# Hybrid HGRN2 / FNet layer: two gate tiles of the conv MLP copied from PSUM to SBUF pages ahead of their conv

## The chip, the cores and the metric

One core of a Trainium2 chip runs the whole program. The time of a run is the device time in microseconds (us); several runs are taken and the median is quoted. A profile is one more execution, with its own time, recorded by the hardware profiler. Engines are called PE (TensorE), PEld (its weight load), DVE (VectorE), ACT (ScalarE), POOL (GpSimd) and SP (SyncE).

## What is computed

One layer on 1024 tokens of width 1024: a token mixer (a gated linear recurrence beside a Fourier mixer), a residual, then a gated MLP with a 3x3 depthwise conv on the gate branch, another residual, and a final RMSNorm. The change lies in the MLP:

```python
def conv_ffn(h, w_up, w_dw, b_dw, w_down, rows, cols):
    a, u = jnp.split(h @ w_up, 2, axis=-1)
    a = lax.conv_general_dilated(a.reshape(B, rows, cols, D_FF), w_dw..., padding=((1, 1), (1, 1)), feature_group_count=D_FF)
    a = a.reshape(B, L, D_FF) + b_dw
    return (jax.nn.gelu(a) * u) @ w_down
```

D_FF is 2816, that is 22 tiles of 128 columns; the grid is 16 rows of 64 tokens.

## The kernel before

Everything is kept transposed: a tile of D_FF columns is 128 partitions by 1024 tokens, gate (`a`) and value (`u`) alike. Each float32 matrix product is made of three matmuls on rounded high and low parts, so every operand is split by `split` (L61 to L63: ACT casts the high part, DVE subtracts it to get the low part).

**Two plain tiles.** The tiles ff = 0 and 1 (`PLAIN = 2`) are computed directly by `plain` (L862), and this work keeps PE busy while norm2 of the second token half is still being made (L745 to L804). The gate columns of such a tile are gathered in a two-bank PSUM tile `psg` (`self.up0[ff][0]`), of which there are two; the value columns go to two one-bank tiles `psm` (four in all) and are copied by ACT to a page `uu` (L803). The gate columns stay in `psg`.

**The twenty other tiles** (loop at L884) use a 2x2 Strassen-like scheme of seven products, each of twelve matmuls (`product`, L854), here named by their weights: A11, A12, S2, S1, S3, S4, A22, in this order on PE. Their sums are closed by ACT copies out of `psm` ("snaps", L889 to L904, recorded at L939) and two DVE additions that write the gate columns into a `psg` tile: L893 (first half, after A12) and L908 (second half, after S4). L893 of tile ff = 2 takes the `psg` buffer that plain tile 0 had, that of ff = 3 the one of tile 1. The second product of a tile, A12, needs a free `psm` buffer; with four of them, A12 of ff = 3 gets the one that L893 of ff = 2 has read.

**The conv** is `gated` (L918): ACT writes the centre tap with the bias into a page `cv` (L922), DVE adds eight shifted taps with scalar_tensor_tensor (L930, in place, 945, 960 or 1008 elements each), reading the gate columns from `psg`; ACT applies gelu (L932), DVE multiplies by `u` (L933) and a DMA stores the page. For the plain tiles the page comes from the common pool `pg` (33 pages of 128x1024), for the others from `cv` (2).

**Loading** of the next tile's weights is `up_load` (L823): DMA, splits on ACT and DVE, and POOL's sums L839 to L842 and the low part L847, which read and write SBUF.

**Order.** The program is written with a tile framework that allots buffers and sets the waits; each engine's queue is ordered at compile time by program order, by readiness in the framework's own forecast, and by the marks `high_priority` (L888 to L911 and L828). On the chip each queue is then worked off strictly in order: what stands behind a waiting instruction waits too.

Of the kernel before, what the change touches and what calls it, by code (L numbers as in the profile page):

```python
# [34 lines left out]
class Kern:  # L35
# [709 lines left out]
    def norm2(self, half, xs, ssacc):  # L745

        nc, V = self.nc, self.nc.vector
        if half == 0:  # L750
            self.B, self.raw = {}, {}
            tag = "g"
        else:
            self.phase("ffn")
            self.upw = [self.up_load(ff) for ff in range(PLAIN)]
            self.up0 = [(self.pst("g"), [self.pst("m")]) for _ in range(PLAIN)]
            self.plain(0, 0, "a")
            tag = "m"
        r = self.token_rstd(ssacc[:, :512], 4, "n2", tag)
        if half:  # L760
            self.plain(0, 0, "u")
        pt = self.pst(tag)
        self.row_bcast(r, 4, pt)
        if half:
            self.plain(1, 0, "au")

        def operand(name, raw=None):
            hi, lo = self.pg(F32R), self.pg(F32R)
            self.B.setdefault(name, []).append((hi, lo))
            if raw is not None:  # L770
                nc.scalar.copy(hi, raw)
                V.tensor_tensor(lo, raw, hi.bitcast(F32), op=SUB)
            return hi, lo

        def block(name, j, kt0):
            raw = self.raw.setdefault(name, {})[j] = self.pg()
            hi, lo = operand(name)
            for i in range(2):
                d = kt0 + i
                q = slice(i * 512, (i + 1) * 512)  # L780
                tmp = self.tile([P, 512], F32, self.tp)
                sh = self.sh2[:, d:d + 1]
                V.scalar_tensor_tensor(tmp, xs[d // 2][:, q], self.a2[:, d:d + 1], pt[:, :512], op0=MUL, op1=MUL)
                nc.scalar.activation(hi[:, q], tmp, AF.Identity, bias=sh)
                V.scalar_tensor_tensor(lo[:, q], tmp, sh, hi[:, q].bitcast(F32), op0=ADD, op1=SUB)
                nc.scalar.activation(raw[:, q], tmp, AF.Identity, bias=sh)
            return raw

        if half == 0:
            for j in range(2):  # L790
                block("B11", j, 2 * j)
            for j in range(2):
                block("B21", j, 4 + 2 * j)
            return
        b12 = [block("B12", j, 2 * j) for j in range(2)]
        b22 = [block("B22", j, 4 + 2 * j) for j in range(2)]
        self.us = []
        for ff in range(PLAIN):
            self.up0[ff][1].append(self.pst("m"))
            self.plain(ff, 1, "au")  # L800
            u = self.pg(F32, "uu")
            for i in range(2):
                nc.scalar.copy(u[:, i * 512:(i + 1) * 512], self.up0[ff][1][i])  # L803
            self.us.append(u)  # L804
        us = []
        for j in range(2):
            u1, u2 = self.pg(F32, "cv"), self.pg()
            V.tensor_tensor(u1, self.raw["B11"][j], b12[j], op=SUB)
            V.scalar_tensor_tensor(u2, u1, -1.0, b22[j], op0=MUL, op1=SUB)
            operand("U2", u2)  # L810
            operand("U1", u1)
            us.append(u2)
        for j in range(2):
            u3 = self.pg(F32, "cv")
            V.tensor_tensor(u3, b22[j], b12[j], op=SUB)
            operand("U3", u3)
        for j in range(2):
            u4 = self.pg(F32, "cv")
            V.scalar_tensor_tensor(u4, us[j], -1.0, self.raw["B21"][j], op0=MUL, op1=SUB)
            operand("U4", u4)  # L820
# [53 lines left out]
    def ffn(self):  # L874
        nc, V = self.nc, self.nc.vector
        self.gd = []
        first = self.tc.high_priority
        h0, h1 = slice(0, 512), slice(512, 1024)
        snap = lambda src, c=1.0: self.copied(self.tile([P, 512], F32, "sn"), src, c)
        self.upw = [self.up_load(PLAIN)]  # L880
        self.B["B12"] = None
        for ff in range(PLAIN):
            self.gated(ff, self.up0[ff][0], self.us[ff])
        for ff in range(PLAIN, NF):  # L884
            w = self.upw.pop(0)
            X, Y = self.pst("m"), self.pst("m")
            self.product(X, w["A11"], "B11", True)
            with first():  # L888
                s1 = snap(X)  # L889
            self.product(Y, w["A12"], "B21", True)  # L890
            pa = self.pst("g")
            with first():
                V.tensor_tensor(pa[:, h0], s1, Y, op=ADD)  # L893
            self.product(X, w["S2"], "U2", False)
            with first():
                sv = snap(X)
            Z = self.pst("m")
            self.product(Z, w["S1"], "U1", True)
            with first():
                s5 = snap(Z)  # L900
            self.product(X, w["S3"], "U3", False)
            u = self.pg(F32, "uu")
            with first():
                s7 = snap(X, -1.0)  # L904
            self.nc.gpsimd.tensor_tensor(u[:, h1], s7, s5, op=SUB)  # L905
            self.product(Z, w["S4"], "B22", False)
            with first():
                V.tensor_tensor(pa[:, h1], sv, Z, op=ADD)  # L908
            self.product(X, w["A22"], "U4", False)
            with first():  # L910
                nc.scalar.mul(u[:, h0], X, -1.0)  # L911
            if ff + 1 < NF:
                self.upw.append(self.up_load(ff + 1))
            self.gated(ff, pa, u)
        self.B = None
        self.down()
# [346 lines left out]


def lay_out(x, c, ctx, c_ctx, w_mod, b_mod, norm1, norm2, w_in, lb_fwd, lb_bwd,
            hgrn_norm, w_out, w_up, w_dw, b_dw, w_down, norm_f):
    A = np.ascontiguousarray
# [45 lines left out]
```

## Time and profile before

| | |
|---|---|
| median of 3 runs | 1223.97 us (1223.35 to 1224.45) |
| the profiled execution's own time | 1221.22 us |
| its span (first to last instruction) | 1219.4 us |
| mean granted TensorE clock, share of full | 0.998 |
| PE busy | 1181.7 us, 97% |
| DVE busy | 917.8 us, 75% |
| ACT busy | 560.2 us, 46% |
| POOL busy | 201.9 us, 17% |

The profiled time lies 2.75 us below the median and 1.8 us above its span. Shares are means over stages of different character: the stage of the change lies between 565 and 680 us of the span, where the plain tiles pass into the loop. A row of the timeline gives start, duration, engine, line, operation, output and input; in brackets stands how long the engine was idle before it and who ended that. Rows that merge several instructions show their count (x4). Successive instructions of an engine overlap a little in the records, so that their spacing is below their duration.

### The profile page before, as it was taken

What the parts mean: (1) busy time and instruction counts of PE and PEld (TensorE: products, weight loads), DVE (VectorE), ACT (ScalarE), POOL (GpSimd) and SP (SyncE); (2) the same over time, 40 slices, a digit from 0 to 9 for tenths busy, and PEclk for the clock granted to TensorE, in tenths of its full rate; (3) what the DMA queues carried; (4) which work ended last, traced back from release to release, by engine and by line L of the source; (5) the groups of instructions that cost most, each with busy time, mean ns of one, the idle gap of its engine ahead of it and who ended that gap; (6) DMA issues with size and microseconds to landing.
All of it is one profiled execution on the core that took longest, in us unless ns stands there. A gap on an engine that the chain in (4) does not pass through costs nothing.

```text
span 1219.4 us, 15862 instructions
## 1 busy us (share of the span) xinstructions
PE 1181.7 (97%) x6156; PEld 989.0 (81%) x6156; DVE 917.8 (75%) x1192; ACT 560.2 (46%) x809; POOL 201.9 (17%) x124
## 2 busy tenths in 40 slices
PE   7999999999998999999999999999999999999997
PEld 4688888888898888888878788888888888788877
DVE  5861858575887467576999888888888898998685
ACT  6534545454431434365544445444443543435552
POOL 0000000000000000001336455464554400000000
PEclk9999999999999999999999999999999999999999
DMA  9531101010246037453022222222212429635643
GB/s 344 224 130 36 35 18 35 18 35 19 87 153 218 10 121 255 168 184 110 19 94 81 110 95 78 87 78 104 87 70 87 141 74 328 243 126 184 211 162 138
DMA packets 57867, 146.23 MB, mean 120 GB/s; under 512 B 5568, under 2 KB 5824, under 8 KB 57792
## 3 DMA queue, kind: packets, MB, share of 16 engines
q1 hardware_dynamic: 57792, 145.22, 34.3%
q8 instruction: 48, 0.79, 0.3%
q14 instruction: 27, 0.22, 0.1%
HBM read 125.27 MB, written 19.92 MB: 119 GB/s over the span
## 4 chain that ended last, share of the span: by engine, by line
PE 62%; DVE 18%; ACT 9%; DMA 5%; issue 5%; SPq 0%; DVEq 0%; ACTq 0%
PE psm L859 24%; PE psm L74 16%; PE psg L74 13%; PE psm L1035 4%; DVE cv L930 4%; PE psg L1035 3%; DVE wl L63 2%; DMA wm<-in_wm_dram 2%; DVE pg L451 1%; DVE pg L930 1%; DVE sl L63 1%; ACT sq L568 1%; ACT L444 1%; ACT L445 1%; DMA ld<-in_wm_dram 1%
## 5 line engine op out<-in xcount | busy, mean ns | idle before, releaser
L930 DVE SCALAR_TENSOR_TENSOR cv<-psg,vec,cv 128x945 f32<-128x945 f32 (+2 forms) x160 | 195.2, 1220 | 24.0 <-ACT cv L922 20.4
L859 PE MATMUL psm<-pg,sh 128*128 128x512 f32 x640 | 197.1, 389 | 0.6 <-ACT sn L939 0.6
L62 ACT CAST wh<-wr 128x1024 fp32r<-128x1024 f32 x78 | 81.9, 1052 | 144.8 <-PE psg L74 39.8
L859 PEld LDWEIGHTS psm<-pg,sh 128*128 128x128 f32 x640 | 120.0, 188 | 25.9 <-ACT sn L939 1.1
L74 PE MATMUL psg<-pg,wh 128*128 128x512 f32 x472 | 134.9, 395 | 0.0
L839 POOL TENSOR_TENSOR ws<-wx 128x512 f32<-128x512 f32 x20 | 28.8, 1441 | 596.4 <-DMA wx<-in_wup_dram 563.1
L63 DVE TENSOR_TENSOR wl<-wr,wh 128x1024 fp32r<-128x1024 f32 x78 | 96.2, 1235 | 40.4 <-ACT wh L62 39.7
L859 PE MATMUL psm<-pg,sl 128*128 128x512 f32 x320 | 124.5, 389 | 0.0
L859 PE MATMUL psm<-pg,wh 128*128 128x512 f32 x320 | 98.6, 389 | 2.8 <-DVE psg L893 2.8
L74 PEld LDWEIGHTS psg<-pg,wh 128*128 128x128 f32 x472 | 87.2, 188 | 16.9
L939 ACT ACTIVATE sn<-psm 128x512 f32<-128x512 f32 x80 | 47.7, 597 | 109.6 <-PE psm L859 109.6
L74 PE MATMUL psg<-wh,pg 128*128 128x256 f32 x512 | 96.4, 287 | 0.9 <-ACT wh L62 0.8
L74 PEld LDWEIGHTS psg<-wh,pg 128*128 128x128 f32 x512 | 80.6, 191 | 1.6 <-ACT wh L62 1.3
L74 PE MATMUL psg<-pg,wl 128*128 128x512 f32 x236 | 79.1, 395 | 0.0
L74 PE MATMUL psg<-wl,pg 128*128 128x256 f32 x256 | 73.0, 286 | 4.4 <-DVE wl L63 4.4
L859 PEld LDWEIGHTS psm<-pg,wh 128*128 128x128 f32 x320 | 60.0, 188 | 15.6 <-DVE psg L893 3.2
L859 PEld LDWEIGHTS psm<-pg,sl 128*128 128x128 f32 x320 | 60.1, 188 | 12.5
L905 POOL TENSOR_TENSOR uu<-sn,sn 128x512 f32<-128x512 f32 x20 | 39.0, 1948 | 180.5 <-ACT sn L939 177.2
L859 PE MATMUL psm<-pg,wl 128*128 128x512 f32 x160 | 62.3, 389 | 0.0
L74 PE MATMUL psm<-pg,pg 128*128 128x128 f32 (+2 forms) x256 | 56.6, 348 | 5.0 <-DVE pg L506 4.7
L221 DVE SCALAR_TENSOR_TENSOR ma<-wm,silu_c,ma 128x512 f32<-128x512 f32 x56 | 42.0, 750 | 18.1 <-DMA wm<-in_wm_dram 17.6
L847 POOL TENSOR_TENSOR sl<-ws,sh 128x1024 fp32r<-128x1024 f32 x20 | 53.4, 2671 | 5.6 <-ACT sh L846 5.6
(376 smaller groups left out, 2622.4 us busy)
## 6 DMA issues: line engine op xcount, KB each, us to landing
wr<-in_wd_dram SPq DMA_DIRECT2D x35, 512.0 KB, 4.0
wm<-in_wm_dram SPq DMA_DIRECT2D x64, 256.0 KB, 2.9
wx<-in_wup_dram SPq DMA_DIRECT2D x22, 512.0 KB, 4.4
wr<-in_wup_dram SPq DMA_DIRECT2D x22, 512.0 KB, 3.6
gd<-cv SPq DMA_DIRECT2D x20, 512.0 KB, 2.6
pg<-gd SPq DMA_DIRECT2D x33, 256.0 KB, 6.2
ld<-in_wm_dram SPq DMA_DIRECT2D x16, 512.0 KB, 8.2
wr<-in_wo_dram SPq DMA_DIRECT2D x16, 512.0 KB, 3.7
```

What stands on the lines that cost most here:

```text
L62: self.nc.scalar.copy(hi, raw)
L63: self.nc.vector.tensor_tensor(lo, raw, hi.bitcast(F32), op=SUB)
L74: self.nc.tensor.matmul(out, lhsT, rhs, start=start, stop=stop)
L221: nc.vector.scalar_tensor_tensor(acc, w, s, acc, op0=MUL, op1=ADD)
L444: nc.scalar.activation(lf, g[d][0], AF.Ln)
L839: G.tensor_tensor(s31[:, hi], u[:, lo], u[:, hi], op=ADD)
L847: G.tensor_tensor(S31[1], s31, S31[0].bitcast(F32), op=SUB)
L859: self.nc.tensor.matmul(out, w[a][:, q], B[kt // 2][b][:, t], start=(first and kt == 0 and j == 0), stop=(kt == 3 and j == 2), skip_group_ ...
L905: self.nc.gpsimd.tensor_tensor(u[:, h1], s7, s5, op=SUB)
L930: V.scalar_tensor_tensor(c3[:, ro, co], a3[:, ri, ci], w9((dr + 1) * 3 + dc + 1), c3[:, ro, co], op0=MUL, op1=ADD)
L939: self.nc.scalar.mul(dst, src, c)
L1035: nc.tensor.matmul(pts[j][:, q], W[a][:, w], G[b][:, i * 512 + q.start:i * 512 + q.stop], start=first and p == 0 and i == 0 and m == 0, st ...
```

## The change

After ACT has copied the value columns of a plain tile, it also copies its gate columns, 128x1024, from `psg` to a page of `pg`, and `gated` of the two plain tiles reads this page in place of `psg`, in L922 and in the eight taps of L930. The references to the tiles are dropped as they are used.

```diff
@@ norm2 @@
             for i in range(2):
                 nc.scalar.copy(u[:, i * 512:(i + 1) * 512], self.up0[ff][1][i])
-            self.us.append(u)
+            a = self.pg()
+            nc.scalar.copy(a, self.up0[ff][0])
+            self.us.append((a, u))
@@ ffn @@
+        self.up0.clear()
         self.upw = [self.up_load(PLAIN)]
         self.B["B12"] = None
         for ff in range(PLAIN):
-            self.gated(ff, self.up0[ff][0], self.us[ff])
+            self.gated(ff, *self.us.pop(0))
```

## Rows read from the trace of the kernel before

**Rows 1.** The page: busy time, share of the span and instructions of PE.
```profile
PE 1181.7 (97%) x6156; PEld 989.0 (81%) x6156; DVE 917.8 (75%) x1192; ACT 560.2 (46%) x809; POOL 201.9 (17%) x124
```

**Rows 2.** PE's waits from 600 us on: us in total, times, longest us.
```profile
PE psm L859 <- DVE psg L893: 2.8, 1, 2.8
PE psm L859 <- ACT sn L939: 2.4, 3, 1.5
```

**Rows 3.** Timeline of PE: A12 and S2 of ff = 3, A22 of ff = 5.
```profile
625.84 0.73 PE L859 MATMUL psm<-pg,wh 128*128 128x512 f32 x2 [2.80 <-DVE psg L893]
...
628.69 0.61 PE L859 MATMUL psm<-pg,sh 128*128 128x512 f32 x2
...
679.33 0.74 PE L859 MATMUL psm<-pg,ah 128*128 128x512 f32 x2 [1.52 <-ACT sn L939]
```

**Rows 4.** Timeline of DVE: the plain tiles' conv, L893 of ff = 2, a later tap.
```profile
604.83 4.56 DVE L930 SCALAR_TENSOR_TENSOR pg<-psg,vec,pg 128x945 f32<-128x945 f32 x4 [1.32 <-ACT pg L922]
...
622.87 2.31 DVE L930 SCALAR_TENSOR_TENSOR pg<-psg,vec,pg 128x945 f32<-128x945 f32 x2
625.11 0.68 DVE L893 TENSOR_TENSOR psg<-sn,psm 128x512 f32<-128x512 f32 x1
...
662.96 1.20 DVE L930 SCALAR_TENSOR_TENSOR cv<-psg,vec,cv 128x945 f32<-128x945 f32 x1 [1.28 <-ACT cv L922]
```

**Rows 5.** Timeline of ACT: idle room, L922 twice, snap, table load and gelu.
```profile
580.76 1.05 ACT L771 CAST pg<-pg 128x1024 fp32r<-128x1024 f32 x1 [1.54 <-DVE pg L809]
...
601.21 1.05 ACT L771 CAST pg<-cv 128x1024 fp32r<-128x1024 f32 x1 [4.48 <-DVE cv L819]
...
603.59 2.31 ACT L922 ACTIVATE pg<-psg,vec 128x1024 f32<-128x1024 f32 x2
605.78 0.59 ACT L939 ACTIVATE sn<-psm 128x512 f32<-128x512 f32 x1
...
624.13 1.28 ACT L932 ACT_TABLE_LOAD   x1 [3.38 <-DVE pg L930]
625.43 1.06 ACT L932 ACTIVATE pg<-pg 128x1024 f32<-128x1024 f32 x1
626.39 0.58 ACT L939 ACTIVATE sn<-psm 128x512 f32<-128x512 f32 x1
...
676.79 1.06 ACT L932 ACTIVATE cv<-cv 128x1024 f32<-128x1024 f32 x1 [3.72 <-DVE cv L930]
```

**Rows 6.** Busy time of PE, PEld, DVE, ACT, POOL in 20 us.
```profile
640.00:660.00 20.00, 20.00 (x90) 16.54 (x89) 19.79 (x18) 9.66 (x13) 10.55 (x7) 1.00 0.29 93
```

**Rows 7.** The conv's taps of 1008 elements, 613 to 616 us: ns min/median/max.
```profile
L930 DVE SCALAR_TENSOR_TENSOR pg<-psg,vec,pg x3: 1260/1260/1260, 612.7 to 615.0; 128x1008 f32<-128x1008 f32 x3
```

**Rows 8.** Timeline of DVE, 592 to 599 us.
```profile
592.08 1.22 DVE L815 TENSOR_TENSOR cv<-pg,pg 128x1024 f32<-128x1024 f32 x1
593.21 1.22 DVE L819 SCALAR_TENSOR_TENSOR cv<-pg,pg 128x1024 f32<-128x1024 f32 x1
594.47 2.20 DVE L772 TENSOR_TENSOR pg<-cv,pg 128x1024 fp32r<-128x1024 f32 x1
596.59 2.31 DVE L63 TENSOR_TENSOR wl<-wr,wh 128x1024 fp32r<-128x1024 f32 x1
```

**Rows 9.** Timeline of POOL, 592 to 626 us.
```profile
592.24 3.35 POOL L839 TENSOR_TENSOR ws<-wx 128x512 f32<-128x512 f32 x1 [23.10 <-DVE sl L63]
595.55 2.27 POOL L842 TENSOR_TENSOR ws<-wr,wx 128x512 f32<-128x512 f32 x1
603.28 2.49 POOL L847 TENSOR_TENSOR sl<-ws,sh 128x1024 fp32r<-128x1024 f32 x1 [5.46 <-ACT sh L846]
...
617.48 1.30 POOL L839 TENSOR_TENSOR ws<-wx 128x512 f32<-128x512 f32 x1 [8.97 <-DVE sl L63]
...
619.99 2.41 POOL L847 TENSOR_TENSOR sl<-ws,sh 128x1024 fp32r<-128x1024 f32 x1
...
624.15 1.27 POOL L841 TENSOR_TENSOR ws<-ws,wr 128x512 f32<-128x512 f32 x1
```

## The prediction

> **What bounds the kernel now.** I read the page first: PE is busy in 97% of the span [rows 1], so only PE's idle time can be won, or added to. Then PE's waits: from 600 us on there are two that count, one of 2.80 us for DVE's L893 and three of 2.4 us together for ACT's snaps, the longest 1.52 us [rows 2]. Then each in its place. The first stands before A12 of ff = 3, at 625.84 [rows 3]. What it waits for is seen on DVE: the 16 taps of the two plain tiles, alternating, begin at 604.83; L893 of ff = 2 stands behind the 15th, at 625.11, because it writes into the `psg` buffer that tile 0's conv has only just finished reading [rows 4]. Its other input, the snap, had ended at 605.78 + 0.59 = 606.37 [rows 5]. The second stands before A22 of ff = 5, at 679.33 [rows 3]: the snap it needs is queued on ACT behind the gelu at 676.79, which had itself waited 3.72 us for conv taps [rows 5]. So in this stretch PE follows DVE, directly or through ACT's queue, and DVE has nothing to spare: 19.79 of 20 us busy from 640 to 660 [rows 6].
>
> **Added: two copies on ACT.** The nearest row is L922, which also reads 128x1024 from `psg`: two in 2.31 us, 1.16 each [rows 5]. The first finds 1.54 us of idle ACT before 580.76, the second 4.48 us before 601.21 [rows 5]; cost nothing. Were that cover gone, 1.16 us would fall before the snap at 605.78. The two pages more come from the pool of 33, in a stage where the operands of the products crowd it; bounds 0 and 2.3 us (two copies' worth of delay to the conv's start), taken as 0, as ACT's idle time before 601.21 is the larger.
>
> **Moved: the buffer comes free at the copy.** L893 of ff = 2 can run at about 607 and L908 when S4 is done, both amid the conv. The 2.80 us before A12 goes. In exchange two DVE instructions of 0.68 us (L908 is of the same kind as L893) now lie ahead of tile 0's last tap [rows 4]; less an overlap of 0.08 each (four taps of 1.2 in 4.56 us are spaced 1.12) that is +1.2 us for its end.
>
> **Changed: the taps read two SBUF operands.** A tap of 1008 elements from `psg` takes 1.26 us [rows 7]; a scalar_tensor_tensor of 1024 with both tensors in SBUF, L819, takes 1.22 [rows 8]. That is at least 0.04 us a tap, about 0.05 at equal length: 16 x 0.05 = 0.8 us of DVE (bounds 0 and 1.0).
>
> **Changed with it: POOL.** Where DVE has two SBUF operands and POOL works at once, both are stretched. POOL's L839 takes 3.35 us at 592.24 but 1.30 at 617.48; L842, 2.27 at 595.55 [rows 9]. DVE's L772 and L63 take 2.20 and 2.31 where L815 and L819 take 1.22 [rows 8]. The ends fit one user at a time: DVE L815, DVE L819 to 594.4, POOL L839 to 595.59, L772 to 596.67, L842 to 597.82, L63 to 598.90. L819 is the tap's own kind of instruction, and L839 made no headway during it. With `psg` as one source there is no such thing: POOL's L847 at 603.28 ran 2.49 us, L847 at 619.99 ran 2.41, and DVE's first four taps beside it kept their spacing of 1.12 [rows 4, 9]. So the change moves 16 taps into the class that collides, in a stretch where POOL has eight instructions, from 603.28 to 624.15 + 1.27 [rows 9].
>
> The Trainium skill ("SBUF — State Buffer", section "SBUF: two separate sides") has it that a DVE instruction with two SBUF inputs and a GpSimd instruction that reads SBUF exclude each other for the whole instruction. The trace agrees at L819, where L839 ended 1.16 us after it, and shows no tap of this kind; by the rule each of the eight would be charged in full, by rows that know taps from `psg` alone none.
>
> The price if they take turns: L847 from the first tap (604.83) to its end at 605.77, 0.94; then L840, L841, L839, L842, L840 at 1.3 each, 6.5; L847, 2.41; in sum 9.85 before tile 0's last tap; the eighth, 1.27, falls about the end of tile 1. The lower bound is that POOL loses whenever DVE has the next tap ready, as it did between L815 and L819, and DVE pays only for what it itself must wait for (0.94, the pair L840 and L841 that its L63 splits, 2.6, and one L847): 5.95. I take turns: of the three handovers in those rows for which both sides stood ready, two went so (L839 to L772 while L842 waited, L772 to L842 while L63 waited).
>
> **What PE loses.** Before, ACT took up the table load at 624.13, on the end of a tap (622.87 + 1.19), then gelu, then the snap of A11 of ff = 3, which ended at 626.97 [rows 4, 5]: 2.91 us from tap to snap. Now that tap ends at 624.06 + 9.85 + 1.2 - 0.75 (15 taps) = 634.4, the snap at 637.3, and S2 of ff = 3, which needs it, starts there and not at 628.69 [rows 3]: +8.6 us, with the 2.80 won before it inside this number. With the lower price that tap ends at 624.06 + 5.95 + 1.2 - 0.75 = 630.5 and S2 starts at 633.4: +4.7. Further on DVE is late by 9.85 + 1.27 - 0.8 = 10.3, less the 1.28 us that it idled before 662.96 [rows 4], so 9.0 at the gelu of 676.79 against PE's 8.6: no second loss worth a term, and nothing is given back. After 680 PE hardly waits [rows 2], so what is lost by then stays.
>
> A POOL instruction that falls beside L893, L908 (both read PSUM) or a wait of DVE costs nothing; I take one of 1.3 us off. Sum: 8.6 - 1.3 = **+7.3 us**. Against the profiled execution that is 1221.22 + 7.3 = 1228.5; the median of the runs lies 2.75 higher, so 1223.97 + 7.3 = 1231.3 us, 0.6% slower.
>
> **The rivals.**
> *No collision, but DVE still bounds.* If taps do not exclude POOL, the 2.80 us are won at 625.84. PE then reaches A22 of ff = 5 earlier by as much and waits there for the same gelu, which depends on DVE alone: the gap grows from 1.52 to 1.52 + 2.80 - 0.8 = 3.5, as DVE's taps save 0.8. Net -0.8 (0 to -1.0), 1223.2: within what can be told, for a measurement of this kernel tells 0.2%, 2.4 us, from no change. For it: taps were never seen colliding. Against: L819.
>
> *The stall goes for good, faster.* Place: ACT's queue. If the framework, with L893 early, sets the snaps of ff = 3 and 5 ahead of the gelus, a late conv no longer holds PE; the two gaps of 2.80 and 1.52 both go, -2.8 to -4.3, 1220.4. It decides where the collision costs DVE under about 2.85 us, one product of PE (625.84 to 628.69 [rows 3]), which is the slack of a snap that goes first. For it: ACT idled 3.38 us before the table load with the snap behind it [rows 5], so the order matters. Against: the order comes from a forecast in which the taps hardly move.
> The Trainium skill ("VectorE: DVE Perf Modes", section "Rules for kernel authors") speaks for it: copy PSUM to SBUF first if many operations follow. No row here shows more than the 0.05 us a tap.
>
> *Turns are taken, but out of the way*: the snaps go ahead of gelu and POOL's lateness meets slack; -2 to +2, 1224.
>
> *Pages.* No collision, but the crowded pool delays U4 or the conv's start by two copies and more: +2.5 to +3, 1227.
>
> **How the numbers follow.** Collision in turns, +4.7 to +8.6: 0.62, since one row shows it for this kind of instruction and four for its neighbours, and as DVE's lateness reaches PE through a queue seen to do so twice. No collision and DVE-bound 0.17; stall gone 0.15; out of the way 0.04; pages 0.02. Slower by over 0.2%: 0.62 + 0.02 = 0.64; within 0.2%: 0.17 + 0.04 = 0.21; faster 0.15. Most chance is of one sign. The range goes up to 8.6 and the 2.3 of the copies' lost cover, less 0.7 as both at once are unlikely, to +10.2, 1234.2, and down through the DVE-bound case to -2, 1222.0; outside lie most of the faster case and little else. The likeliest case's own range is 1228.6 to 1232.6.
>
> **What would show it.** In the changed kernel's profile: no PE wait for L893 near 625; L893 at 606 to 610; taps `pg<-pg,vec,pg` with durations of 2 us and more beside POOL's L840, L841, L839, and those stretched beyond 1.3; the last tap of tile 0 near 634; a PE wait for ACT's snap of 8 to 11 us near 628 to 638. Wrong, if the taps keep to 1.2 us beside a busy POOL: then a gap of about 3.5 us at 679 speaks for the first rival, none for the second.

## The result and the profile after

The changed kernel takes 1244.16 us (median of 5 runs, 1242.65 to 1245.04) against 1224.45 us for the kernel before beside it: a ratio of 1.0155, 95% interval [1.0139, 1.0171]. That is slower, as forecast, but by 19.7 us and not by 7.3, and outside the range. The changed kernel's profiled execution took 1242.65 us, its span 1240.8. Lines of `plain` and `gated` have moved by two or three: L922 is now L925, the taps L930 are L933, L932 is L935, L893 is L896, L908 is L911, the snaps L939 are L942, L859 is L861, L809 is L811, POOL's L839 to L842 are L841 to L844, and the copy is L805.

First, engine totals and PE's waits. From the page (busy us, share of span, instructions):

```profile
PE 1189.6 (96%) x6156; PEld 994.2 (80%) x6156; DVE 923.7 (74%) x1192; ACT 561.2 (45%) x811; POOL 207.2 (17%) x124
```

and PE's waits from 600 us on (us in total, times, longest us):

```profile
PE psm L861 <- ACT sn L942: 11.2, 7, 3.8
PE psm L861 <- DVE psg L911: 4.2, 1, 4.2
...
PE psm L861 <- DVE pg L772: 0.8, 1, 0.8
```

Beside [rows 1], PE is busy 7.9 us longer with the same 6156 instructions; beside [rows 2], the waits in the loop are 11.2 + 4.2 + 0.8 = 16.2 us in place of 5.2, so 11.0 more. The wait for L893 is gone; the waits for snaps have taken its place, and there are seven. Part of the longer span (1240.8 against 1219.4) I do not count to the change: the last work that both kernels do in the same order, DVE's first L808 or L810, starts at 577.71 before and at 580.96 after, 3.25 us later. In the profiles of the ten experiments below it starts between 579.40 and 583.69, at 580.58 in e8, whose program differs from the kernel before only behind it. Part of the extra PE time lies in that start too.

Why PE waits is read first from DVE, whose queue has changed most. Before, in a timeline (start, duration, engine, line, operation, tiles; idle before in brackets), U2's second instruction, L809, follows the first at once:

```profile
577.71 1.23 DVE L808 TENSOR_TENSOR cv<-pg,pg 128x1024 f32<-128x1024 f32 x1
...
579.51 1.22 DVE L809 SCALAR_TENSOR_TENSOR pg<-cv,pg 128x1024 f32<-128x1024 f32 x1
```

After, in the same view:

```profile
580.96 1.21 DVE L810 TENSOR_TENSOR cv<-pg,pg 128x1024 f32<-128x1024 f32 x1
...
588.21 1.23 DVE L63 TENSOR_TENSOR wl<-wr,wh 128x1024 fp32r<-128x1024 f32 x1 [4.25 <-ACT wh L62]
593.66 1.23 DVE L63 TENSOR_TENSOR sl<-ws,sh 128x1024 fp32r<-128x1024 f32 x1 [4.22 <-ACT sh L62]
594.80 1.22 DVE L811 SCALAR_TENSOR_TENSOR pg<-cv,pg 128x1024 f32<-128x1024 f32 x1
599.09 1.23 DVE L63 TENSOR_TENSOR wl<-wr,wh 128x1024 fp32r<-128x1024 f32 x1 [3.08 <-ACT wh L62]
...
613.32 0.68 DVE L896 TENSOR_TENSOR psg<-sn,psm 128x512 f32<-128x512 f32 x1
...
623.36 2.17 DVE L933 SCALAR_TENSOR_TENSOR pg<-pg,vec,pg 128x945 f32<-128x945 f32 x1 [0.21 <-ACT pg L925]
...
626.05 4.91 DVE L933 SCALAR_TENSOR_TENSOR pg<-pg,vec,pg 128x960 f32<-128x960 f32 x2
...
653.43 3.32 DVE L933 SCALAR_TENSOR_TENSOR pg<-pg,vec,pg 128x945 f32<-128x945 f32 x1
```

L811's input, the `cv` of L810, is ready at 582.2, yet in DVE's queue L811 now stands behind two weight splits (L63) that wait for ACT's casts (L62). DVE idles 4.25 + 4.22 + 3.08 = 11.55 us, the operands U2 to U4 come late, and the first tap starts at 623.36; before, it started at 604.83 [rows 4]. The same in windows of the changed kernel (us, then busy time and count of PE, PEld, DVE, ACT, POOL, granted clock, DMA share, GB/s); DVE is busy 8.46 of the first 20 us, where in the kernel before it was busy 19.96:

```profile
580.00:600.00 20.00, 20.00 (x90) 16.56 (x89) 8.46 (x9) 7.82 (x11) 3.46 (x2) 1.00 0.09 27
...
640.00:660.00 20.00, 13.58 (x48) 10.36 (x48) 17.88 (x14) 6.32 (x7) 11.77 (x6) 0.83 0.00 0
649.70:655.00 5.30, 5.23 (x13) 4.14 (x14) 5.30 (x5) 2.68 (x4) 5.30 (x3) 0.54 0.00 0
...
661.00:666.00 5.00, 4.86 (x14) 3.88 (x15) 3.93 (x4) 3.21 (x6) 1.67 (x1) 0.66 0.52 195
...
691.00:696.00 5.00, 4.73 (x14) 3.74 (x15) 4.93 (x5) 2.06 (x4) 0.00 (x0) 0.66 0.08 30
```

DVE loses the time before 600, but PE pays for most of it from 645 on, in three stops. Its timeline there:

```profile
649.77 1.22 PE L861 MATMUL psm<-pg,wh 128*128 128x512 f32 x2 [4.17 <-DVE psg L911]
661.14 1.00 PE L861 MATMUL psm<-pg,sh 128*128 128x512 f32 x2 [3.39 <-ACT sn L942]
691.27 0.73 PE L861 MATMUL psm<-pg,sh 128*128 128x512 f32 x2 [3.77 <-ACT sn L942]
```

PE is stopped in three ways. The first stop waits for L911, which stands on DVE behind the taps. The other two wait for snaps, and ACT's timeline shows what held them:

```profile
660.49 0.60 ACT L942 ACTIVATE sn<-psm 128x512 f32<-128x512 f32 x1 [6.35 <-POOL uu L908]
...
689.53 1.20 ACT L925 ACTIVATE cv<-psg,vec 128x1024 f32<-128x1024 f32 x1 [6.60 <-DMA gd<-cv]
```

The snap at 660.49 waited for POOL's L908. L908 was the last of six POOL instructions in a row, begun at 648.08 behind a late DVE split. Four of them took 2.17, 2.19, 3.40 and 2.07 us beside DVE, where the same four take 1.30, 1.30, 2.41 and 1.28 us undisturbed in the kernel before: 3.5 us more. The snaps before 691.27 stood behind a centre tap that waited for the store of an earlier conv page. The prediction has neither of these two ways.

After each of these three stops the windows above show a low granted clock, 0.54 and twice 0.66 of 2.4 GHz, so for the greater part the lower level of 1.2 GHz. The kernel before ran 23 matmuls in 5.16 us behind its 2.80 us stop, 0.224 us each, at a granted clock of 1.00:

```profile
625.80:631.00 5.20, 5.16 (x23) 4.28 (x24) 4.87 (x6) 4.70 (x6) 1.30 (x1) 1.00 0.76 299
```

At that rate the 13, 14 and 14 matmuls of the three windows would have taken 2.9, 3.1 and 3.1 us; they took 2.3 + 1.7 + 1.6 = 5.6 us more. So each of these stops was paid for twice: as idle time, and as slow matmuls after it.

### The profile page after: what moved, and what is told of

The parts are those of the page before. It is cut to its first block, busy times and chain, and to the rows that moved or that the text cites. A ratio compares the mean times of both kernels' runs of the same rounds, so it can differ in the third digit from the quotient of the medians.

```text
span 1240.8 us, 15849 instructions
## 1 busy us (share of the span) xinstructions
PE 1189.6 (96%) x6156; PEld 994.2 (80%) x6156; DVE 923.7 (74%) x1192; ACT 561.2 (45%) x811; POOL 207.2 (17%) x124
## 4 chain that ended last, share of the span: by engine, by line
PE 58%; DVE 15%; ACT 9%; DMA 7%; issue 6%; POOL 4%; SPq 1%; DVEq 0%; ACTq 0%; POOLq 0%
PE psm L861 21%; PE psm L74 15%; PE psg L74 13%; PE psm L1038 4%; PE psg L1038 3%; DVE cv L933 3%; DMA wm<-in_wm_dram 3%; DVE wl L63 1%; POOL sl L849 1%; DVE pg L451 1%; DMA wr<-in_wd_dram 1%; DVE sl L63 1%; ACT sq L568 1%; ACT L444 1%; DMA ld<-in_wm_dram 1%
## 5 line engine op out<-in xcount | busy, mean ns | idle before, releaser
L933 DVE SCALAR_TENSOR_TENSOR cv<-psg,vec,cv 128x945 f32<-128x945 f32 (+2 forms) x160 | 193.9, 1219 | 24.4 <-ACT cv L925 21.4
L861 PE MATMUL psm<-pg,sh 128*128 128x512 f32 x640 | 200.2, 394 | 9.5 <-ACT sn L942 8.7
L861 PEld LDWEIGHTS psm<-pg,sh 128*128 128x128 f32 x640 | 121.3, 190 | 36.7 <-ACT sn L942 10.4
L62 ACT CAST wh<-wr 128x1024 fp32r<-128x1024 f32 x78 | 82.0, 1052 | 151.0 <-PE psg L74 44.0
L841 POOL TENSOR_TENSOR ws<-wx 128x512 f32<-128x512 f32 x20 | 28.5, 1427 | 623.7 <-DMA wx<-in_wup_dram 565.8
L63 DVE TENSOR_TENSOR wl<-wr,wh 128x1024 fp32r<-128x1024 f32 x78 | 95.0, 1219 | 47.1 <-ACT wh L62 46.0
L861 PE MATMUL psm<-pg,sl 128*128 128x512 f32 x320 | 125.7, 393 | 0.0
L861 PE MATMUL psm<-pg,wh 128*128 128x512 f32 x320 | 99.6, 393 | 4.2 <-DVE psg L911 4.2
L942 ACT ACTIVATE sn<-psm 128x512 f32<-128x512 f32 x80 | 47.4, 595 | 107.8 <-PE psm L861 101.4
L861 PEld LDWEIGHTS psm<-pg,wh 128*128 128x128 f32 x320 | 60.5, 189 | 17.1 <-DVE psg L911 4.6
L861 PEld LDWEIGHTS psm<-pg,sl 128*128 128x128 f32 x320 | 60.9, 190 | 12.9
L908 POOL TENSOR_TENSOR uu<-sn,sn 128x512 f32<-128x512 f32 x20 | 37.2, 1861 | 168.3 <-ACT sn L942 154.9
L861 PE MATMUL psm<-pg,wl 128*128 128x512 f32 x160 | 62.7, 392 | 0.0
L221 DVE SCALAR_TENSOR_TENSOR ma<-wm,silu_c,ma 128x512 f32<-128x512 f32 x56 | 42.0, 749 | 19.7 <-DMA wm<-in_wm_dram 19.3
```

The source lines that it names most:

```text
L62: self.nc.scalar.copy(hi, raw)
L63: self.nc.vector.tensor_tensor(lo, raw, hi.bitcast(F32), op=SUB)
L221: nc.vector.scalar_tensor_tensor(acc, w, s, acc, op0=MUL, op1=ADD)
L841: G.tensor_tensor(s31[:, hi], u[:, lo], u[:, hi], op=ADD)
L861: self.nc.tensor.matmul(out, w[a][:, q], B[kt // 2][b][:, t], start=(first and kt == 0 and j == 0), stop=(kt == 3 and j == 2), skip_group_ ...
L933: V.scalar_tensor_tensor(c3[:, ro, co], a3[:, ri, ci], w9((dr + 1) * 3 + dc + 1), c3[:, ro, co], op0=MUL, op1=ADD)
```

## The experiments

Two theories stood after this. **Pages**: the copies' page requests stand ahead of U2's in the common pool, and this turns DVE's queue over. **Collision**: the taps that read two SBUF operands lose time to POOL, as forecast. Ratios are against runs of the kernel before on the same chip (1224.2 to 1225.5 us).

### The place of the copies, and what the taps read

Both copies late, behind the operands U1 to U4 in the program, in place of the early ones; the taps read the pages (e1):

```diff
@@ norm2, behind U4 @@
+        for ff in range(PLAIN):
+            a = self.pg()
+            nc.scalar.copy(a, self.up0[ff][0])
+            self.us[ff] = (a, self.us[ff])
```

> As the changed kernel, but the two copies stand behind the operands U1 to U4 in the program, so their pages are asked for last. Page theory (the early request for two pages holds up the pages of U2 and all behind it, and DVE loses some 12 us before the conv): the DVE idle time between 584 and 600 us is gone, the taps begin at about 605 as before the change, and what stays is the collision of the taps with GpSimd, 5 to 9 us over the kernel before, 1229 to 1233 us. Collision theory (nearly all of the 20 us is the taps waiting for GpSimd and the clock falling on it): 14 to 19 us over, 1238 to 1243 us.

Both copies early, as in the change; only L922 reads the page, the taps read `psg` (e2):

```diff
-            self.gated(ff, *self.us.pop(0))
+            self.gated(ff, self.up0[ff][0], self.us[ff][1], self.us[ff][0])
@@ gated(ff, pa, u, mid=None) @@
-        nc.scalar.activation(cv, pa, AF.Identity, ...)
+        nc.scalar.activation(cv, pa if mid is None else mid, AF.Identity, ...)
```

> As the changed kernel, pages asked for early and held until the centre tap reads them, but the eight shifted taps read the PSUM tile again, so that they do not collide with GpSimd (and the PSUM tile stays held to the end of the conv). Page theory: DVE idles some 12 us between 584 and 600 again, taps begin near 620, and 9 to 13 us over the kernel before, 1233 to 1238 us. Collision theory: within 3 us of the kernel before, 1223 to 1228 us.

Both copies late, and taps from `psg`: e1 and e2 together (e7).

> Both copies late, the centre tap reads the pages, the eight shifted taps read PSUM. It differs from the run with both copies late and taps from SBUF in the taps' source and in what follows from it (the PSUM tiles are held to the end of the conv). Collision theory: tap durations are 1.19 to 1.26 us throughout, and the time is within 2 us of the kernel before, 1223.5 to 1227.5 us. If the late copies themselves (2 us on ACT ahead of the first snap) are what costs: 1228 to 1231 us, as with the taps from SBUF.

| copies | taps from the page | taps from `psg` |
|---|---|---|
| early | the change: 1244.16 us, 1.0155 [1.0139, 1.0171] | e2: 1238.70 us, 1.0107 [1.0073, 1.0142] |
| late | e1: 1229.81 us, 1.0036 [1.0020, 1.0052] | e7: 1229.69 us, 1.0040 [1.0027, 1.0053] |

The place of the copies is worth 0.7 to 1.2% (8 to 15 us), what the taps read 0.5% with early copies (the two intervals just touch) and nothing with late ones. DVE's busy time from 580 to 600 goes with the place: 19.96 us in e1, as before the change, and 9.10 in e2:

```profile
580.00:600.00 20.00, 20.00 (x90) 16.54 (x90) 9.10 (x10) 7.82 (x12) 3.46 (x2) 1.00 0.08 26
```

So the place of the copies carries most of the loss, as the pages theory has it. The collision is real all the same. In e1, with U1 to U4 made as before, taps that meet POOL are stretched (two in 4.38 us; undisturbed, two take 2.31 [rows 4]); in e7 they keep their spacing.

```profile
628.38 4.38 DVE L935 SCALAR_TENSOR_TENSOR pg<-pg,vec,pg 128x945 f32<-128x945 f32 x2
```

The two then pay in different places, as PE's timelines show, e1 (first) in ACT's queue and e7 (second) for `psg`, which is freed late as before:

```profile
633.54 1.22 PE L863 MATMUL psm<-pg,sh 128*128 128x512 f32 x2 [6.22 <-ACT sn L944]
```

```profile
631.33 1.22 PE L863 MATMUL psm<-pg,wh 128*128 128x512 f32 x2 [6.56 <-DVE psg L897]
```

With late copies this is a draw: the early free `psg` seems to win what the collision costs. I had expected e7 at 1223.5 to 1227.5 if the collision were e1's whole price; at 1229.69 it is not. Late copies have a price of their own, seen on ACT in e7: they stand ahead of the first snap and the centre taps, and DVE waits 3.65 us for its first tap in place of 1.32 [rows 4].

```profile
605.68 1.93 ACT L823 COPY pg<-psg 128x1024 f32<-128x1024 f32 x2
607.49 0.62 ACT L943 ACTIVATE sn<-psm 128x512 f32<-128x512 f32 x1
607.97 2.39 ACT L926 ACTIVATE pg<-pg,vec 128x1024 f32<-128x1024 f32 x2
```

To see this alone, both copies were made late to pages that nothing reads (e9):

```diff
+        for ff in range(PLAIN):
+            nc.scalar.copy(self.pg(), self.up0[ff][0])
```

> The kernel before with both gate tiles copied late to pages that nothing reads: centre tap and shifted taps read PSUM. It leaves the copies' time on ACT, and nothing else of the change. In the run with late copies and taps from PSUM the conv began about 2.3 us late and the wait for L893 was 6.6 us in place of 2.8. If that came from the copies' 2 us on ACT ahead of the snap and the centre taps: the same here, 2.5 to 5 us over the kernel before, 1227.5 to 1230 us. If it came from the centre tap's reading of the pages: 0 to 1.5 us over.

Measured 1233.72, 1.0072 [1.0046, 1.0097]. The stage is that of e7 (first tap at 609.37, PE's wait 6.52 at 631.43), so the copies' time on ACT is enough for e7's loss; but e9 is some 4 us slower than e7 and above what was expected, in part in small waits spread behind the stage. The two intervals overlap, and that remainder is not explained.

### Which copy, how many pages, or whose pool

Tile 0's copy early and tile 1's late, behind U4 (e5); the other way round (e6). Shown is the early place alone:

```diff
+            if ff == 0:        # e6: ff == 1
+                a = self.pg()
+                nc.scalar.copy(a, self.up0[ff][0])
+                u = (a, u)
```

> Both tiles copied and read from SBUF, as in the changed kernel, but only the copy of tile 0 stands before the operands U1 to U4 in the program, that of tile 1 behind them. If a page asked for early holds up the requests behind it until the copy that fills it is ready: tile 0's gate columns are done at about 587 us, so DVE idles only 2 to 4 us before the pages of U2 come, and the time is that of the run with both copies late (+4 us) plus 0 to 3, 1229 to 1233 us. If one page fewer is what matters: about as far over as the next run, 1236 to 1240 us.

> The mirror image: only the copy of tile 1 stands before the operands. Its gate columns are done at about 598 us. If the early request holds up those behind it: DVE idles about 12 us between 584 and 600 as in the changed kernel, and the time is 1238 to 1244 us. If one page fewer is what matters: as the previous run.

e5 took 1235.55, 1.0090 [1.0066, 1.0113], more than the order of requests was to cost and a little less than one page fewer was to, with one long idle time on DVE (3.11 us) and the second U2 operand at 591.45. e6 took 1244.60, 1.0159 [1.0135, 1.0182]: tile 1's copy alone brings back the whole loss, and DVE's timeline has the same idle times as the change:

```profile
589.06 1.23 DVE L63 TENSOR_TENSOR wl<-wr,wh 128x1024 fp32r<-128x1024 f32 x1 [4.25 <-ACT wh L62]
594.51 1.22 DVE L63 TENSOR_TENSOR sl<-ws,sh 128x1024 fp32r<-128x1024 f32 x1 [4.22 <-ACT sh L62]
595.65 1.22 DVE L813 SCALAR_TENSOR_TENSOR pg<-cv,pg 128x1024 f32<-128x1024 f32 x1
599.94 1.22 DVE L63 TENSOR_TENSOR wl<-wr,wh 128x1024 fp32r<-128x1024 f32 x1 [3.07 <-ACT wh L62]
```

Tile 1's copy is the later to be filled. In the changed kernel ACT makes the two at

```profile
588.09 1.00 ACT L805 COPY pg<-psg 128x1024 f32<-128x1024 f32 x1
...
598.97 1.00 ACT L805 COPY pg<-psg 128x1024 f32<-128x1024 f32 x1
```

Is it that the pool has two pages fewer to give? The kernel before, with no copy and 31 pages (e3):

```diff
-BUFS = dict(cst=1, sm=2, pg=33, wr=2, wh=2, wl=2)
+BUFS = dict(cst=1, sm=2, pg=31, wr=2, wh=2, wl=2)
```

> The kernel before with 31 common pages in place of 33, nothing copied. If it is the number of pages that is short, DVE idles between 580 and 600 us as in the changed kernel and the time is 8 to 13 us over the kernel before. If it is the order of the requests (the pages of the copies, asked for ahead of the operands, hold up all behind them until the second tile's gate columns are done), two pages fewer cost 0 to 3 us.

Measured 1228.75, 1.0025 [1.0009, 1.0040]; L893's wait is 4.05 us, and DVE is busy 19.93 us from 580 to 600:

```profile
580.00:600.00 20.00, 20.00 (x90) 16.57 (x89) 19.93 (x21) 13.78 (x18) 1.67 (x1) 1.00 0.08 26
```

The number is worth 3 us, not 19. Last, the change as it is, with both copies early, but their pages from a pool of their own and 31 in the common one, the same memory (e10):

```diff
-            a = self.pg()
+            a = self.tile([P, 1024], F32, "ga")
-BUFS = dict(cst=1, sm=2, pg=33, wr=2, wh=2, wl=2)
+BUFS = dict(cst=1, sm=2, pg=31, ga=2, wr=2, wh=2, wl=2)
```

> The change as made, both copies early in the program, but their pages come from a pool of their own (two pages), and the common pool has 31 in place of 33, so that the memory is the same. Theory (the copies' page requests stand ahead of U2's in the common pool's order and hold them up): with the requests in another pool U2's operands are made in time again, DVE is busy 19 to 20 of 20 us from 580 to 600 as with 31 pages alone, the first tap is back at 605 to 612, and the time is 1226 to 1233 (31 pages alone gave +3.1 us, both copies late +4.3). Rival (the early copies themselves, by their work on ACT or by the PSUM buffers that they free early, turn the queues over): DVE 580 to 600 stays at 8 to 12 us busy, first tap near 623, 1240 to 1246.

Measured 1229.06, 1.0026 [1.0013, 1.0039]. The window and DVE's timeline of e10:

```profile
580.00:600.00 20.00, 20.00 (x90) 16.55 (x89) 19.83 (x17) 13.83 (x16) 4.43 (x2) 1.00 0.08 27
```

```profile
580.25 1.22 DVE L810 TENSOR_TENSOR cv<-pg,pg 128x1024 f32<-128x1024 f32 x1
...
582.05 1.22 DVE L811 SCALAR_TENSOR_TENSOR pg<-cv,pg 128x1024 f32<-128x1024 f32 x1
...
605.02 9.96 DVE L933 SCALAR_TENSOR_TENSOR pg<-ga,vec,pg 128x945 f32<-128x945 f32 x5
...
626.33 3.82 DVE L933 SCALAR_TENSOR_TENSOR pg<-ga,vec,pg 128x1008 f32<-128x1008 f32 x2
630.07 3.36 DVE L936 TENSOR_TENSOR pg<-pg,uu 128x1024 f32<-128x1024 f32 x1
```

U2's second instruction is back at 582.05 and the first tap at 605.02, with the same copies at the same place in the program. So the early work on ACT, the early free `psg` and the taps' source are not what turned DVE's queue over: that the copies ask the common pool for their pages, ahead of U2, is. How the pool comes to put L811 behind the splits is inferred, from e3 (not the number of pages) and from e5 and e6 (worse for the page that is filled later): the trace shows the finished order of a queue, and not which page a request waited for when it was made. On the chip L811 does not wait for tile 1's copy: it runs at 594.80, the copy at 598.97. If the requests hold it up, they do so where the order is made, at compile time.

### One copy, and none

Only tile 0's gate columns copied, late (e4): 1224.71, 0.9991 [0.9976, 1.0006], no difference.

```diff
+        a = self.pg()
+        nc.scalar.copy(a, self.up0[0][0])
+        self.up0[0] = (a, self.up0[0][1])
```

> Only the gate columns of plain tile 0 are copied, late, and only its eight taps read SBUF; tile 1 stays in PSUM. The 2.8 us wait for the first PSUM tile goes, half the taps collide. Page theory with half the collision: 0 to 4 us over the kernel before, 1224 to 1228 us; if the early PSUM tile is worth more than eight colliding taps cost, 1 to 3 us under it. Collision theory: 6 to 10 us over.

What the change frees early is tile 0's `psg`, which L893 of ff = 2 waits for. The same can be had without a copy: the kernel before alternates the taps of the two tiles, so tile 0's last tap comes 15th or 16th. Here tile 1's conv is queued behind tile 0's last tap, which `gated` now returns (e8):

```diff
-        for ff in range(PLAIN):
-            self.gated(ff, self.up0[ff][0], self.us[ff])
+        tap = self.gated(0, self.up0[0][0], self.us[0])
+        with self.tc.issue_after(tap.ins):
+            self.gated(1, self.up0[1][0], self.us[1])
```

> The kernel before, nothing copied, but DVE's queue is told to take tile 1's taps after those of tile 0 in place of alternating. Tile 0's PSUM tile is then free about 616 us, L893 of ff = 2 comes before PE needs its buffer, and the 2.8 us wait goes without copies. If DVE bounds the stretch as a whole, the wait comes back later and the time is within 1.5 us of the kernel before; if not, 2 to 4 us under it, 1221.5 to 1223.5 us.

Measured 1221.09, 0.9970 [0.9958, 0.9981]: better than both kernels. DVE's timeline has L894 (L893 of before) at 619.74, behind nine taps and not fifteen; PE's waits from 600 us on hold no wait for it:

```profile
607.68 3.69 DVE L931 SCALAR_TENSOR_TENSOR pg<-psg,vec,pg 128x945 f32<-128x945 f32 x3 [1.31 <-ACT pg L923]
...
612.42 7.40 DVE L931 SCALAR_TENSOR_TENSOR pg<-psg,vec,pg 128x1008 f32<-128x1008 f32 x6
619.74 0.68 DVE L894 TENSOR_TENSOR psg<-sn,psm 128x512 f32<-128x512 f32 x1
```

```profile
PE psm L859 <- ACT sn L941: 3.4, 3, 1.4
```

Its conv begins 607.68 - 604.83 [rows 4] = 2.85 us later than that of before, and its span of 1218.9 us still ends 0.5 us earlier: 3.4 us gained behind the conv's start, of the 4.0 us by which the medians differ. Of these, 5.2 [rows 2] less 3.4 = 1.8 us are waits of the loop; the rest was not traced.

## Why the prediction was wrong

**The failed step** is this one, on the pages: "The two pages more come from the pool of 33, in a stage where the operands of the products crowd it; bounds 0 and 2.3 us (two copies' worth of delay to the conv's start), taken as 0, as ACT's idle time before 601.21 is the larger." The first tap came at 623.36 instead of 604.83. Even without the 3.25 us by which everything was late, that is 623.36 - 604.83 - 3.25 = 15.3 us, over six times the upper bound. Two things were wrong in it. The bound was the time of two copies, while the delay came from a queue in another order: L811 behind splits for which DVE idled 11.55 us. And ACT's idle time says when ACT could copy, not who asks for pages behind the copies. Nor could the first of the two idle times be used. PE's timeline of the kernel before has the last matmuls into the gate columns of tile 0 and tile 1:

```profile
583.65 0.39 PE L74 MATMUL psg<-pg,wl 128*128 128x512 f32 x1
...
594.53 0.39 PE L74 MATMUL psg<-pg,wl 128*128 128x512 f32 x1
```

They end at 584.04 and 594.92, the first behind the 580.76 that the text names, both behind U2's start at 577.71. So these rows could show that the copies are filled late, and the program that their pages are asked for ahead of U2's. The rival *Pages* had the right place at 0.02 and a price (+2.5 to +3) that fits e3's two pages fewer and not the order of requests.

**The copies on ACT at nothing**: right for the early place. In e10 they are there and the first tap stands 605.02 - 580.25 = 24.8 us behind the first L810; before, 604.83 - 577.71 = 27.1 us behind L808. Late, without that cover, they take 1.93 us ahead of the first snap and the centre taps, seen in e7 and e9; the text had named 2.3 for its loss.

**The collision in turns, 9.85 + 1.27 us, less 1.3**: right in kind; in size it was near only with what it took from other instructions than the taps. In e10 the stretched instructions, against 1.12 us a tap in a row and 1.21 for L936, are 9.96 - 5.7 = 4.3, 3.82 - 2.4 = 1.4, one tap of 2.24 us for 1.0, and L936, 3.36 - 1.2 = 2.2: 8.9 us for 9.8 forecast, 6.7 of them in taps. In the change itself it is 7.2 us: 2.17 for 1.0 above an undisturbed tap, 4.91 for 2.6, 5.64 for 1.1, 1.63 for 0.4 and 3.32 for 2.1. That POOL's own lateness could stop PE, as at 661.14, was not in the sum.

**From DVE to PE**: the way through ACT's queue was right, the size not. e10 has PE's wait for a snap where the text put it, 7.21 us at 634.66 (forecast: 8 to 11 near 628 to 638):

```profile
634.66 1.22 PE L861 MATMUL psm<-pg,sh 128*128 128x512 f32 x2 [7.21 <-ACT sn L942]
```

But e10 loses 3.2 us (1.0026), not 7.3, and 31 pages alone cost as much (e3, 1.0025); whether it is the same loss was not tested. Taking off the 2.5 us by which its stage began later (580.25 against 577.71), S2 comes 634.66 - 628.69 [rows 3] - 2.5 = 3.5 us late, below even my lower price of 4.7. The sum had kept DVE's old order, with tile 0's last tap behind 15 others; in e10's queue tile 0's taps come sooner, the table load and gelu find them done at 625.84, ahead of half of the collision, and the snap waits instead behind ACT's L914 for the L936 that POOL stretched:

```profile
633.52 0.60 ACT L914 ACTIVATE uu<-psm 128x512 f32<-128x512 f32 x1 [5.01 <-DVE pg L936]
```

**The wait for L893**: gone, as forecast; L896 at 613.32 and not 606 to 610, since it lies behind the late operands. In e10, with the operands on time, it starts at 614.90, behind five taps that meet POOL.

**The clock**: not in the sum at all. I took a PE stop at its own length. 5.6 us of the loss are matmuls at a lower granted clock behind three stops.

By the profile, the changed kernel lost 1240.8 - 1219.4 - 3.25 = 18.2 us behind the start of its stage: 11.0 in waits and 5.6 by the clock, with 1.6 not traced. The direction was right by luck: by e10 against e3 the collision that I gave for it is worth about nothing beside what the early `psg` wins, and the loss comes with the early requests for pages, which the sum had at nothing. Only on top of these does the taps' source cost something, 0.5% from e2 to the change.

## What to carry to other kernels

Before a tile is taken earlier from a pool that others share, look in the program at who asks next. Here two requests that were filled late put the operands behind them out of order, at a price far above the copies' own 2.0 us; a pool of their own or a later place avoided it (19.7 us, 3.2 with the own pool). Look also for the order that frees the buffer without a copy; letting tile 0's taps go first gained 4 us where the copy lost 20. And price a stop of PE with the matmuls behind it, not by its length alone.

## What was not expected of the hardware

The granted clock after a stop. Behind 2.80 us of idle PE it was 1.00 (23 matmuls in 5.16 us); behind 3.39 and 3.77 us it was 0.66 (14 in 4.86 and in 4.73 us), behind 4.17 us 0.54 (13 in 5.23 us). e10 shows it behind 7.21 us:

```profile
634.60:640.00 5.40, 5.34 (x17) 4.30 (x18) 5.40 (x5) 1.42 (x3) 3.78 (x2) 0.73 0.50 149
```

The price was 2.3, 1.7 and 1.6 us for the three stops of the changed kernel, and 5.34 - 17 x 0.224 = 1.5 us for the one of e10: it did not grow with the length of the stop. The Trainium skill ("TensorE: Matmul & The Clock Gate", section "Part 1: The HAM clock gate") has a gate that runs the array at half its clock when it has been idle and at the full one when it has been busy; these windows agree, with 0.54 to 0.73 behind four stops and 1.00 behind the shortest.

The collision reaches further than the taps, as [rows 8, 9] had shown of L772 and L63: DVE's L936, a tensor_tensor of two SBUF pages, took 3.36 us beside POOL in e10 where it takes 1.21 alone (L933 at 627.41 in the kernel before). And an ACT copy of 128x1024 from `psg` takes 1.00 us, shorter than the 1.16 that I had taken from L922.
